# The high parts of split weights loaded by a second, rounding transfer that GpSimd issues

## The chip, the cores and the metric

The kernel runs on one core of a Trainium2 chip. A core has five engines with an instruction stream each, executed in order: TensorE (PE in the profile, its weight loads PEld), VectorE (DVE), ScalarE (ACT), GpSimd (POOL) and SyncE (SP), which in this kernel issues the transfers. Engines wait for each other on semaphores. The metric is the device time of one execution in microseconds.

## What is computed

One layer of a hybrid block over 512 latent and 256 context tokens, width 2048, in float32:

```python
h  = rms_norm(x, norm_w) * (1 + scale) + shift            # shift, scale, gate from silu(c) @ w_ada + b_ada
hc = rms_norm(ctx, norm_w) * (1 + scale_c) + shift_c      # the same from c_ctx
qkv_g, z_g, gates, q_a, k_a, v_a, z_a = split_proj(h @ w_in)      # w_in: 2048 x 6688
qkv_gc, ..., k_ac, v_ac, _            = split_proj(hc @ w_in)
# group A: 8 heads of a gated delta rule, chunks of 64, one scan forwards and one backwards,
#   first over the context, then over the latent tokens; conv of 5 taps and silu on q, k, v
o_gdn   = o_lf + flip(o_lb)
gdn_lat = rms_norm(o_gdn, gdn_norm_w) * silu(z_g)
# group B: 8 query heads, 2 key/value heads, rotary positions
attn_lat = block_attention(qa, k_all, v_all) * silu(z_a)
y = concatenate([gdn_lat, attn_lat]) @ w_out              # w_out: 2048 x 2048
out = rms_norm(x + gate * y, final_norm_w)
```

## The kernel before, in words

**Products in three passes.** The matrix products with `w_in` and `w_out` are made with operands rounded to `float32r` (F32R). To keep the accuracy, each operand is split in a high part (the value rounded to F32R) and a low part (the value less its high part), and the product is the sum of three: high x high, high x low, low x high. `hhL` and `hL` are the high and low part of `h`, `hhC` and `hC` those of `hc`, `mh` and `ml` those of the gated head outputs.

**Pieces of weights.** Weights come in pieces of 256 KB, 128 partitions x 512. A piece of `w_in` is 512 rows and 128 columns, so it is read in runs of 512 bytes; one of `w_out` is 128 rows of 512 columns, runs of 2 KB. `wpiece` allots the three tiles of a piece (`wraw`, `whi`, `wlo`, three buffers each), has SP load `wraw` (L138), and calls `split`: ACT copies `wraw` to `whi`, which rounds (L129, a CAST in the profile), and `lo_eng` subtracts (L130). `lo_eng` is VectorE (V) for 236 pieces, all but the first weights.

**Stages.** Start (to about 170 us): loading `w_ada`, the modulation, `h` and the first head's projections; its weights go through `first_weights` with GpSimd subtracting (16 pieces `wraw_w`). Scans (about 170 to 870 us): per head `gdn_scan` goes through 12 steps, and PE fills the steps' waits with the projections of the next heads, `feeding` with `proj_steps`: 24 pieces for k, 24 for q, 28 for v, 16 for the attention's keys and values (`kv`), 32 for its queries (`q0a` and so on) and 20 for gates (`z..a`). A step: `ksh` (PE, state times key), `rh` (DVE, L866), `tsh` (PE, L875), `vsh` and `vnh` (ACT, L879 and L882), `tsh` (PE, L886), `sth` (DVE, L892, the new state, which adds `sdh`, the decayed state that POOL makes, L240). Beside the scan of one head `gdn_prep` prepares the next: `cch`, `grh`, `IB`, `NTh`, `NEh` are its tiles, `cacc_k` and `cacc_q` the convolutions, `kq` and `kc` their results. Attention and gates (about 870 to 1112 us): scores, softmax and values per head, with the other 44 pieces of gate columns (`z_piece`, `fillers`, output `zl`) as PE's filler; `ptl` and `qTl` are low parts that DVE makes there. Output (about 1112 to 1302 us): four blocks of 512 columns, 16 pieces each; blocks 0 to 2 through `wpiece` (48 pieces, `wraw_wo`, output `po`), block 3 from its own tiles `rawl`, `wlh`, `wll`, loaded and split during blocks 1 and 2. `epilogue` adds each block into `yx` (`tt`, `yx`).

**What sets the order.** PE's order is that of the program, in all stages; in attention and gates DVE, ACT and POOL follow the program too. In the scans and the output a list scheduler orders the other engines from its own estimates of durations, with priorities (`first_of_all`, `soon`). A changed engine or duration of one instruction can therefore move others.

Of the kernel before, what the change touches and what calls it, by code (L numbers as in the profile page):

```python
# [9 lines left out]
F32R = mybir.dt.float32r  # L10
AF = mybir.ActivationFunctionType
ALU = mybir.AluOpType
# [56 lines left out]
def build(tc, a):  # L69
    nc = tc.nc  # L70
    V, S, G, T, SY = nc.vector, nc.scalar, nc.gpsimd, nc.tensor, nc.sync
# [4 lines left out]
    def pool(name, bufs=1, **kw):  # L76
        return es.enter_context(tc.tile_pool(name=name, bufs=bufs, **kw))
# [4 lines left out]
    wp = pool("wp", 1)  # L82
# [43 lines left out]
    def split(raw, nm, lo_eng=None):  # L126
        hi = wp.tile([128, 512], F32R, tag="whi", bufs=3, name=f"whi_{nm}")
        lo = wp.tile([128, 512], F32R, tag="wlo", bufs=3, name=f"wlo_{nm}")
        S.copy(hi, raw)  # L129
        (lo_eng or G).tensor_tensor(out=lo, in0=raw, in1=hi, op=ALU.subtract)  # L130
        return hi, lo

    def wpiece(src, nm, shape, lo_eng=None):
        raw = wp.tile([128, 512], F32, tag="wraw", bufs=3, name=f"wraw_{nm}")
        v = raw
        if shape is not None:
            v = raw.rearrange("p (a b) -> p a b", b=shape)
        SY.dma_start(v, src)  # L138
        hi, lo = split(raw, nm, lo_eng)
        if shape is not None:  # L140
            hi = hi.rearrange("p (a b) -> p a b", b=shape)
            lo = lo.rearrange("p (a b) -> p a b", b=shape)
        return hi, lo
# [10 lines left out]
    def proj_steps(col, nm, pl, pc=None):  # L154


        for kq in range(4):
            src = w_in[kq * 512:(kq + 1) * 512, col:col + 128].rearrange("(k p) c -> p k c", p=128)
            hi, lo = wpiece(src, f"{nm}_{kq}", 128, V)
            passes = [(kq * 4 + k4, n, lw, rt) for k4 in range(4)  # L160
                      for n, (lw, rt) in enumerate(hpass(kq * 4 + k4, hi[:, k4], lo[:, k4]))]

            def one(out, m, k, n, lw, rt):
                T.matmul(out, lhsT=lw, rhs=rt[m], start=k == 0 and n == 0, stop=k == KT - 1 and n == 2,  # L164
                         skip_group_check=True)

            if pc is not None and kq == 0:
                for out, m, n_ in ((pl, 0, SEQ), (pc, 1, CTX)):
                    for x in passes:
                        one(out, m, *x)  # L170
                        yield n_
                continue
            for x in passes:
                one(pl, 0, *x)
                if pc is not None:
                    one(pc, 1, *x)
                yield SEQ if pc is None else SEQ + CTX
# [196 lines left out]
    def first_weights(k):  # L374

        rows = w_in[k * 128:(k + 1) * 128]
        src = rows[:, 0:2048].rearrange("p (s c) -> p s c", s=2)[:, :, 0:256]
        hi, lo = wpiece(src, f"w0_{k}", 256)
        raw, vhi, vlo = [p0.tile([128, 128], t_, tag=i, bufs=3, name=f"{i}{k}")
                         for i, t_ in (("w0r", F32), ("w0h", F32R), ("w0l", F32R))]  # L380
        SY.dma_start(raw, rows[:, COL_V:COL_V + 128])
        S.copy(vhi, raw)
        G.tensor_tensor(out=vlo, in0=raw, in1=vhi, op=ALU.subtract)
        w0[k] = (hi[:, 0], vhi, hi[:, 1]), (lo[:, 0], vlo, lo[:, 1])
# [953 lines left out]
    def z_piece(n):  # L1338
        i, kq = zs[n // 4], n % 4
        col = (COL_ZG if i < 8 else COL_ZA - 1024) + i * 128  # L1340
        src = w_in[kq * 512:(kq + 1) * 512, col:col + 128].rearrange("(k p) c -> p k c", p=128)
        return wpiece(src, f"z{i}_{kq}", 128, V)
# [189 lines left out]
    for c in range(4):  # L1532
# [9 lines left out]
        for k in range(KT):  # L1542
            hi = op_.tile([128, 512], F32R, name=f"wlh{k}")
            lo = op_.tile([128, 512], F32R, name=f"wll{k}")
            raw = op_.tile([128, 512], F32, tag="rawl", bufs=2, name=f"rawl{k}")
# [4 lines left out]
        for t in range(4):  # L1550
# [5 lines left out]
            f = fr[:, t:t + 1]  # L1556
# [36 lines left out]
```

## Time and profile before

| | |
|---|---|
| three runs | 1307.06, 1307.14, 1307.84 us; median 1307.14 |
| the profiled execution, its span | 1304.42 us, 1302.6 us |
| TensorE clock granted | 0.993 of full speed |
| busy: PE, DVE, ACT, POOL | 1250.4, 842.5, 583.4, 141.9 us |
| traffic | 164.53 MB, mean 126 GB/s |
| the 236 pieces' raw loads, 256 KB each | landing 2.8 to 3.3 us after issue (medians by kind) |
| low parts on DVE (L130) | 0.69 us each |

The profile is one execution, in microseconds from the span's start. A row of a group names line, engine, operation, output<-inputs and shape, then how often, busy time and mean duration in ns, and after a bar the idle time of that engine just before, with what ended it. A row of a timeline has start and duration first. Tile names stand without buffer and head numbers.

### The profile page before, as it was taken

The page shows a single profiled execution, that of the slowest core. Times are in us where ns is not written, and L with a number is a line of the kernel's source. Part 1 is how long each engine was busy: PE and PEld are TensorE (multiplying, and loading weights), DVE is VectorE, ACT ScalarE, POOL GpSimd, SP SyncE. Part 2 cuts the span into 40 slices and gives each one's busy share as a digit, 9 for nine tenths or more (in the row PEclk, how much of TensorE's full clock was granted, in tenths as well). Part 3 has the DMA queues.
Part 4 walks back from the last instruction along what each step waited for, and adds up shares of the span by engine and source line. Part 5 has one row for each costly group of instructions (what it writes and reads, how often), then busy time and mean ns, then how long its engine had stood idle before and what let it go on. Part 6 is the DMA issues. An engine that isn't in the chain of part 4 may idle for free. (4 is left out here: it accounts for less than half of the span.)

```text
span 1302.6 us, 24348 instructions
## 1 busy us (share of the span) xinstructions
PE 1250.4 (96%) x9226; PEld 1018.4 (78%) x9226; DVE 842.5 (65%) x1893; ACT 583.4 (45%) x1464; POOL 141.9 (11%) x206
## 2 busy tenths in 40 slices
PE   6799999999999999999999999999999999999997
PEld 4466688888888888888888877787888888788885
DVE  5444596686867678675776646537888887555432
ACT  4222363455545454544545444535555444434211
POOL 1323100111111111111111001100000000000000
PEclk9999999999999999999999999999999999999998
DMA  9999424231332313222132443356443443475302
GB/s 354 316 326 347 133 67 107 60 67 55 74 72 62 78 47 83 67 69 57 54 83 75 106 131 110 99 164 214 149 129 114 123 140 102 161 244 190 93 33 97
DMA packets 227000, 164.53 MB, mean 126 GB/s; under 512 B 62210, under 2 KB 198491, under 8 KB 225859
## 3 DMA queue, kind: packets, MB, share of 16 engines
q1 hardware_dynamic: 226586, 162.87, 42.9%
q8 instruction: 73, 1.20, 0.4%
q14 instruction: 44, 0.36, 0.1%
q10 hardware_dynamic: 297, 0.11, 0.0%
HBM read 148.85 MB, written 14.08 MB: 125 GB/s over the span
## 5 line engine op out<-in xcount | busy, mean ns | idle before, releaser
L240 POOL TENSOR_TENSOR sdh<-sth,egl 128x256 f32<-128x256 f32 x80 | 56.9, 711 | 446.6 <-DVE sth L892 344.8
L871 ACT ACTIVATE oqh<-ksh,egsw 64x128 f32<-64x128 f32 x128 | 46.3, 362 | 92.7 <-DVE rh L866 86.4
L866 DVE SCALAR_TENSOR_TENSOR rh<-ksh,negeg,vtokh 64x128 f32<-64x128 f32 x176 | 61.2, 348 | 31.1 <-PE ksh L854 24.5
L146 PE MATMUL po<-whi_wo,mh 128*128 128x512 f32 x192 | 76.2, 397 | 0.0
L148 PE MATMUL po<-whi_wo,ml 128*128 128x512 f32 x192 | 76.1, 396 | 0.0
L147 PE MATMUL po<-wlo_wo,mh 128*128 128x512 f32 x192 | 76.1, 396 | 0.0
L1361 PE MATMUL zl<-hhL,whi_z 128*128 128x512 f32 x176 | 74.0, 421 | 0.0
L1361 PE MATMUL zl<-hhL,wlo_z 128*128 128x512 f32 x176 | 69.8, 396 | 0.0
L1361 PE MATMUL zl<-hL,whi_z 128*128 128x512 f32 x176 | 69.6, 395 | 0.0
L130 DVE TENSOR_TENSOR wlo_wo<-wraw_wo,whi_wo 128x512 fp32r<-128x512 f32 x48 | 33.0, 690 | 55.5 <-ACT whi_wo L129 55.3
L886 PE MATMUL tsh<-vsh,ktok 128*128 128x128 f32 x352 | 56.6, 283 | 6.7 <-ACT vnh L882 3.5
L886 PEld LDWEIGHTS tsh<-vsh,ktok 128*128 128x128 f32 x352 | 47.4, 190 | 16.0 <-ACT vnh L882 7.9
L129 ACT CAST whi_wo<-wraw_wo 128x512 fp32r<-128x512 f32 x48 | 29.6, 620 | 67.3 <-PE po L148 56.8
L892 DVE TENSOR_TENSOR sth<-sdh,tsh 128x256 f32<-128x256 f32 x80 | 33.6, 420 | 27.4 <-PE tsh L886 19.2
L879 ACT ACTIVATE vsh<-tsh,cch 128x128 f32<-128x128 f32 x88 | 32.2, 366 | 38.4 <-PE tsh L875 37.1
L164 PE MATMUL vl<-hhL,wlo_v 128*128 128x512 f32 x112 | 46.3, 413 | 0.0
L164 PE MATMUL vl<-hhL,whi_v 128*128 128x512 f32 x112 | 46.2, 413 | 0.0
L164 PE MATMUL vl<-hL,whi_v 128*128 128x512 f32 x112 | 45.8, 409 | 0.0
L1402 DVE SCALAR_TENSOR_TENSOR gacc<-graw,scol,gacc 128x512 f32<-128x512 f32 x60 | 44.9, 748 | 1.0
L950 ACT CAST pth<-pt 128x512 fp32r<-128x512 f32 x48 | 26.8, 585 | 40.7 <-PE pt L1289 40.7
L146 PEld LDWEIGHTS po<-whi_wo,mh 128*128 128x128 f32 x192 | 36.2, 188 | 9.5 <-ACT whi_wo L129 0.8
L148 PEld LDWEIGHTS po<-whi_wo,ml 128*128 128x128 f32 x192 | 36.2, 189 | 8.7
(540 smaller groups left out, 3890.2 us busy)
## 6 DMA issues: line engine op xcount, KB each, us to landing
wada<-in_w_ada SPq DMA_DIRECT2D x64, 512.0 KB, 8.6
graw<-in_w_ada SPq DMA_DIRECT2D x64, 256.0 KB, 3.1
wraw_wo<-in_w_out SPq DMA_DIRECT2D x48, 256.0 KB, 3.3
wraw_z<-in_w_in SPq DMA_DIRECT2D x44, 256.0 KB, 3.1
wraw_v<-in_w_in SPq DMA_DIRECT2D x28, 256.0 KB, 2.9
wraw_k<-in_w_in SPq DMA_DIRECT2D x24, 256.0 KB, 2.9
wraw_q<-in_w_in SPq DMA_DIRECT2D x24, 256.0 KB, 2.8
xs<-in_x SPq DMA_DIRECT2D x4, 1024.0 KB, 5.4
```

Source lines behind the costliest of these rows:

```text
L130: (lo_eng or G).tensor_tensor(out=lo, in0=raw, in1=hi, op=ALU.subtract)
L146: T.matmul(out, lhsT=lh, rhs=rh, start=start, stop=False, skip_group_check=True)
L147: T.matmul(out, lhsT=lh, rhs=rl, start=False, stop=False, skip_group_check=True)
L148: T.matmul(out, lhsT=ll, rhs=rh, start=False, stop=stop, skip_group_check=True)
L164: T.matmul(out, lhsT=lw, rhs=rt[m], start=k == 0 and n == 0, stop=k == KT - 1 and n == 2, skip_group_check=True)
L240: eng.tensor_tensor(out=out, in0=x, in1=y, op=ALU.mult)
L866: V.scalar_tensor_tensor(out=r[rows], in0=ks[rows, d], scalar=gsc["negeg"][rows, gcol:gcol + 1], in1=vtok[rows, p], op0=ALU.mult, op1=ALU.add)
L871: S.activation(oq[rows, v, p - 2], ks[rows, d], AF.Copy, scale=gsc["egsw"][rows, gcol:gcol + 1])
L886: T.matmul(ts[:, d], lhsT=ktok[:, p, half], rhs=vs, start=True, stop=True, skip_group_check=True)
L892: V.tensor_tensor(out=sn, in0=sd, in1=ts[:, 0:2], op=ALU.add)
L1361: T.matmul(pl, lhsT=lw, rhs=rt, start=k == 0 and m == 0, stop=k == KT - 1 and m == 2, skip_group_check=True)
L1402: V.scalar_tensor_tensor(out=acc, in0=raw, scalar=scol[:, k:k + 1], in1=acc, op0=ALU.mult, op1=ALU.add)
```

## The change

In `wpiece`, when VectorE makes the low part, the high part is no longer a copy of `wraw` by ScalarE. GpSimd issues a second transfer of the same 256 KB from the weights in DRAM into the `whi` tile, which rounds to F32R on the way. The subtraction stays on VectorE, and needs both transfers. The pieces of the first weights are as before. 236 pieces are concerned, in scans, z projections and the output's first three blocks.

```diff
     def wpiece(src, nm, shape, lo_eng=None):
         raw = wp.tile([128, 512], F32, tag="wraw", bufs=3, name=f"wraw_{nm}")
-        v = raw
+        hi = wp.tile([128, 512], F32R, tag="whi", bufs=3, name=f"whi_{nm}")
+        lo = wp.tile([128, 512], F32R, tag="wlo", bufs=3, name=f"wlo_{nm}")
+        v, u = raw, hi
         if shape is not None:
-            v = raw.rearrange("p (a b) -> p a b", b=shape)
+            v, u = [t.rearrange("p (a b) -> p a b", b=shape) for t in (raw, hi)]
         SY.dma_start(v, src)
-        hi, lo = split(raw, nm, lo_eng)
+        if lo_eng is V:
+            G.dma_start(u, src)
+        else:
+            S.copy(hi, raw)
+        (lo_eng or G).tensor_tensor(out=lo, in0=raw, in1=hi, op=ALU.subtract)
         if shape is not None:
             hi = hi.rearrange("p (a b) -> p a b", b=shape)
             lo = lo.rearrange("p (a b) -> p a b", b=shape)
```

All lines behind it move down by 6 (L886 becomes L892, L892 becomes L898). PE's order stays, but for six rows in one piece of the first output block. ACT loses 236 instructions, POOL gains as many, and the scheduler places DVE's work in the scans and the output anew.

VectorE in the scan of head 1, while head 3's q projection runs (`q3_2` and `q3_3` are its last two pieces). Before, the third piece's low part stands ahead of the convolution:

```order
L240 TENSOR_TENSOR cch2_3601<-cch2_3601,esuf_86 128x12
L130 TENSOR_TENSOR wlo_q3_2_3781<-wraw_q3_2_3778,whi_q3_2_3780 128x512
L221 SCALAR_TENSOR_TENSOR cacc_k3_3627<-craw2_1554,cvT_78,cacc_k3_3627 128x512
L221 SCALAR_TENSOR_TENSOR cacc_k3_3627<-craw2_1554,cvT_78,cacc_k3_3627 128x256
L221 SCALAR_TENSOR_TENSOR cacc_k3_3627<-craw2_1554,cvT_78,cacc_k3_3627 128x512
L892 TENSOR_TENSOR sth1_2_3687<-sdh1_2_3611,tsh1_2_3651 128x256
```

The fourth follows one step later, before `grh`:

```order
L892 TENSOR_TENSOR sth1_3_3788<-sdh1_3_3703,tsh1_3_3771 128x256
L240 TENSOR_TENSOR IB0_1638<-gqh2_3661,grh2_3500 64x4x64
L130 TENSOR_TENSOR wlo_q3_3_3813<-wraw_q3_3_3810,whi_q3_3_3812 128x512
L702 TENSOR_TENSOR grh2_3500<-grh2_3500,cch2_3601 128x768
L866 SCALAR_TENSOR_TENSOR rh1_4_3797<-ksh1_3483,negeg_85,vtokh1_2803 64x128 x2
```

Now both stand one step further down:

```order
L246 TENSOR_TENSOR IB0_1638<-gqh2_3661,grh2_3500 64x4x64 x4
L898 TENSOR_TENSOR sth1_3_3788<-sdh1_3_3703,tsh1_3_3771 128x256
L708 TENSOR_TENSOR grh2_3500<-grh2_3500,cch2_3601 128x768
L145 TENSOR_TENSOR wlo_q3_2_3780<-wraw_q3_2_3778,whi_q3_2_3779 128x512
L246 TENSOR_TENSOR grh2_3500<-gqh2_3661,grh2_3500 128x256 x2
L246 TENSOR_TENSOR grh2_3500<-gch2_3715,grh2_3500 128x128 x2
L724 STREAM_TRANSPOSE NTh2_3504<-grh2_3500 32x6x32 x3
L872 SCALAR_TENSOR_TENSOR rh1_4_3797<-ksh1_3483,negeg_85,vtokh1_2803 64x128 x2
L724 STREAM_TRANSPOSE NTh2_3504<-grh2_3500 32x6x32
L145 TENSOR_TENSOR wlo_q3_3_3812<-wraw_q3_3_3810,whi_q3_3_3811 128x512
```

`wlo_q3_2` went from ahead of `sth1_2` to behind `sth1_3`, past all of `cacc_k3`, `kq3`, `kc3`, `IB0` and the first `grh`; `wlo_q3_3` from ahead of `grh` to behind `rh1_4` and the transposes.

GpSimd at the same place, before (`vinh` and `sdh` are its only work there):

```order
L240 TENSOR_TENSOR sdh1_2_3611<-sth1_1_3573,egl_88 128x256
L671 TENSOR_TENSOR vinh2_3598<-skh2_3590,expo2_79 128x6
L240 TENSOR_TENSOR sdh1_3_3703<-sth1_2_3687,egl_88 128x256
L240 TENSOR_TENSOR sdh1_4_3800<-sth1_3_3788,egl_88 128x256
L240 TENSOR_TENSOR sdh1_5_3863<-sth1_4_3833,egl_88 128x256
```

and now:

```order
L246 TENSOR_TENSOR sdh1_2_3611<-sth1_1_3573,egl_88 128x256
L677 TENSOR_TENSOR vinh2_3598<-skh2_3590,expo2_79 128x6
L142 DMA whi_q3_2_3779<-in_w_in 128x4x128
L246 TENSOR_TENSOR sdh1_3_3703<-sth1_2_3687,egl_88 128x256
L142 DMA whi_q3_3_3811<-in_w_in 128x4x128
L142 DMA whi_v3_0_3852<-in_w_in 128x4x128
L246 TENSOR_TENSOR sdh1_4_3800<-sth1_3_3788,egl_88 128x256
L142 DMA whi_v3_1_3907<-in_w_in 128x4x128
L246 TENSOR_TENSOR sdh1_5_3863<-sth1_4_3833,egl_88 128x256
```

Each transfer waits there until PE has freed its `whi` buffer, and the `sdh` behind it waits with it.

VectorE where the output's second block begins, before:

```order
L130 TENSOR_TENSOR wlo_wo1_1_12990<-wraw_wo1_1_12987,whi_wo1_1_12989 128x512
L240 TENSOR_TENSOR tt0_0_12941<-po0_0_12572,gbc_12931 128x512
L240 TENSOR_TENSOR tt0_1_12946<-po0_1_12573,gbc_12931 128x512
L1528 TENSOR_TENSOR yx_12930<-yx_12930,tt0_0_12941 128x512
L1528 TENSOR_TENSOR yx_12930<-yx_12930,tt0_1_12946 128x512
L130 TENSOR_TENSOR wlo_wo1_2_13008<-wraw_wo1_2_13005,whi_wo1_2_13007 128x512
```

and now:

```order
L145 TENSOR_TENSOR wlo_wo1_1_12989<-wraw_wo1_1_12987,whi_wo1_1_12988 128x512
L1554 TENSOR_TENSOR wll0_13598<-rawl0_13599,wlh0_13597 128x512
L246 TENSOR_TENSOR yx_12930<-yx_12930,fwb_12932 128x512 x2
L246 TENSOR_TENSOR tt0_2_12951<-po0_2_12574,gbc_12931 128x512
L246 TENSOR_TENSOR tt0_3_12956<-po0_3_12575,gbc_12931 128x512
L1534 TENSOR_TENSOR yx_12930<-yx_12930,tt0_2_12951 128x512
L1534 TENSOR_TENSOR yx_12930<-yx_12930,tt0_3_12956 128x512
L145 TENSOR_TENSOR wlo_wo1_2_13007<-wraw_wo1_2_13005,whi_wo1_2_13006 128x512
```

`wlo_wo1_1` went behind the first two `tt` and `yx`, and `wlo_wo1_2` behind the rest of the first block's epilogue and one `wll`.

## The prediction

> **What bounds the kernel now.** I read the page first: the busy shares and the chain that ended last.
>
> ```profile
> PE 1250.4 (96%) x9226; PEld 1018.4 (78%) x9226; DVE 842.5 (65%) x1893; ACT 583.4 (45%) x1464; POOL 141.9 (11%) x206
> PE 30%; DVE 4%; issue 2%; ACT 2%; DMA 0%; SPq 0%; POOL 0%; POOLq 0%; DVEq 0%; ACTq 0%
> ```
>
> TensorE (PE) works 96% of 1302.6 us, so work taken from ScalarE (ACT), 45% busy, buys at most what PE waits for through ACT. The chain says the same: ACT 2%, DMA 0%. PE's waits, by what ended them, give that ceiling (columns: total us, times, longest).
>
> ```profile
> PE tsh L886 <- ACT vnh L882: 3.5, 6, 1.0
> PE tsh L886 <- ACT vsh L879: 3.0, 5, 0.9
> PE kvl L164 <- DVE wlo_kv L130: 2.1, 1, 2.1
> ```
>
> PE is late by ACT in the scans for 3.5 + 3.0 = 6.5 us, and by a low part once (2.1 us); no row names a `whi`. So the 236 casts cost PE almost nothing today. The groups tell what they feed (columns: busy, mean ns, idle before and its releaser).
>
> ```profile
> L129 ACT CAST whi_wo<-wraw_wo 128x512 fp32r<-128x512 f32 x48 | 29.6, 620 | 67.3 <-PE po L148 56.8 <-PE zl L1361 8.7 <-ACT tt L1529 0.9
> L130 DVE TENSOR_TENSOR wlo_wo<-wraw_wo,whi_wo 128x512 fp32r<-128x512 f32 x48 | 33.0, 690 | 55.5 <-ACT whi_wo L129 55.3
> L130 DVE TENSOR_TENSOR wlo_z<-wraw_z,whi_z 128x512 fp32r<-128x512 f32 x44 | 30.2, 688 | 13.0 <-ACT whi_z L129 13.0
> L240 POOL TENSOR_TENSOR sdh<-sth,egl 128x256 f32<-128x256 f32 x80 | 56.9, 711 | 446.6 <-DVE sth L892 344.8 <-DVE sth L890 48.2 <-DVE msh L906 23.7
> L892 DVE TENSOR_TENSOR sth<-sdh,tsh 128x256 f32<-128x256 f32 x80 | 33.6, 420 | 27.4 <-PE tsh L886 19.2 <-ACT NTq L937 2.2 <-ACT NTh L649 1.9
> L130 POOL TENSOR_TENSOR wlo_w<-wraw_w,whi_w 128x512 fp32r<-128x512 f32 x16 | 22.1, 1382 | 34.4 <-ACT whi_w L129 34.4
> ```
>
> A cast lasts 0.62 us and starts when PE frees the `whi` buffer (56.8 us of the 67.3 in the output). POOL idles before `sdh`, and `sth` waits for PE, not for `sdh`: POOL has slack.
>
> **Part 1, the casts go.** 236 x 0.62 = 146 us of ACT disappear. On PE's path lie at most the 6.5 us above, and most of those instructions stand behind copies that stay. I take -4; ends -6.5 and 0.
>
> **Part 2, the price of a high part.** It came 0.62 us after PE's release, from a raw tile already there. Now POOL issues a transfer after that release. No row shows a POOL issue; the nearest are SP's issue and transfers of equal size.
>
> ```profile
> 1149.50 0.33 SPq L138 DMA_DIRECT2D wraw_wo<-in_w_out  x1
> wraw_wo<-in_w_out SPq DMA_DIRECT2D x48, 256.0 KB, 3.3
> wraw_v<-in_w_in SPq DMA_DIRECT2D x28, 256.0 KB, 2.9
> yx<-in_x SPq DMA_DIRECT2D x16, 256.0 KB, 4.4
> wraw_w<-in_w_in SPq DMA_DIRECT2D x16, 256.0 KB, 8.3
> ```
>
> An issue takes between 0.33 us and POOL's longest instruction here, 1.38 (`wlo_w`); I take 1.0, as software work on POOL is nearer to its own instructions. Landing: at best 2.9, at worst 8.3 (a row from the start, where the DMA engines are full). I take 3.3 + (1.0 - 0.33) = 4.0 us from release. The 236 x 0.25 MB = 59 MB (MB as 2^20) more bring the share up, but from a low level:
>
> ```profile
> 170.00:870.00 700.00, 683.30 (x6176) 573.37 (x6176) 480.53 (x1219) 345.67 (x977) 92.88 (x134) 1.00 0.32 80
> 870.00:1112.00 242.00, 236.84 (x1319) 198.56 (x1318) 188.35 (x312) 116.82 (x261) 8.49 (x7) 1.00 0.46 140
> 1112.00:1246.00 134.00, 134.00 (x572) 107.10 (x571) 66.48 (x104) 50.51 (x94) 0.00 (x0) 1.00 0.51 165
> ```
>
> Columns from the third: busy us of PE, PEld, DVE, ACT, POOL, then clock, DMA share, GB/s. The output stage goes from 165 to about 165 + 48 x 0.262 MB / 134 us = 259 GB/s, a share near 0.8; the scans stay below 0.5. The issues cost POOL 148 x 1.0 us in 700 us where it works 93: hidden, but for `sdh` that queues behind a transfer waiting for its buffer, which costs some `sth` up to a us. I take +1, ends 0 and +5.
>
> [...]
>
> **Part 3, the low parts move on DVE.** This is the main term. PE's order is fixed, DVE executes in order, and in the changed order `wlo_q3_2` stands behind a whole block of convolution and `IB` work, and behind `sth1_3` and `grh`. The rows around it before:
>
> ```profile
> 330.50 0.68 DVE L130 TENSOR_TENSOR wlo_q<-wraw_q,whi_q 128x512 fp32r<-128x512 f32 x1
> ...
> 340.32 0.42 DVE L892 TENSOR_TENSOR sth<-sdh,tsh 128x256 f32<-128x256 f32 x1
> ...
> 341.23 0.75 DVE L130 TENSOR_TENSOR wlo_q<-wraw_q,whi_q 128x512 fp32r<-128x512 f32 x1
> 341.91 0.95 DVE L702 TENSOR_TENSOR grh<-grh,cch 128x768 f32<-128x768 f32 x1
> ...
> 344.81 1.57 DVE L718 STREAM_TRANSPOSE NTh<-grh 32x192 f32<-32x192 f32 x4
> 339.70 0.48 PE L164 MATMUL ql<-hhL,wlo_q 128*128 128x512 f32 x1
> 343.04 0.39 PE L164 MATMUL ql<-hhL,wlo_q 128*128 128x512 f32 x1
> ```
>
> Before, `wlo_q3_2` ran at 330.50, 9 us ahead of PE's need at 339.70. After, the work between them is the same, `grh` takes the place at 341.23 that `wlo_q3_3` leaves, and `wlo_q3_2` starts behind it at 341.23 + 0.95 = 342.2 and ends at 342.9: PE stands 3.2 us. Its high part is not what is late: its cast had ended before 330.50, so with the 4.0 us of part 2 it lands by about 335. `wlo_q3_3`, now behind the rest of `grh`, the transposes and `rh1_4`, comes after 344.81 + 1.57, less its own 0.75 that is gone from 341.23, plus 0.69 of `wlo_q3_2`, and ends 0.68 later: 347.0, with small gaps 347.3. PE needed it at 343.04: 4.3 us late in all, the 3.2 included.
>
> The head 7 order is word for word the same; head 4 is alike.
>
> ```profile
> 648.53 0.42 DVE L892 TENSOR_TENSOR sth<-sdh,tsh 128x256 f32<-128x256 f32 x1
> 651.25 0.39 PE L164 MATMUL ql<-hhL,wlo_q 128*128 128x512 f32 x1
> 413.97 0.68 DVE L130 TENSOR_TENSOR wlo_q<-wraw_q,whi_q 128x512 fp32r<-128x512 f32 x1
> 424.11 0.37 DVE L718 STREAM_TRANSPOSE NTh<-grh 32x192 f32<-32x192 f32 x1
> 421.07 0.39 PE L164 MATMUL ql<-hhL,wlo_q 128*128 128x512 f32 x1
> ```
>
> Head 7 is the same distances 308.2 us later: +4.3. In head 4, `wlo_q4_2` moves from 413.97 to behind the transposes that end at 424.48, less the 0.42 of `sth` that now follows it: it ends at about 424.7 against a need at 421.07, +3.6, of which a little may be regained: 3.4. Sum 12.0. Other pieces (kv1, q2, q5, q6) move by fewer places, each 0 to 1.5 us late: +2.5, ends 0 and +5. Bounds of part 3: 0, if PE regains each stall in later waits (it has 17 us of idle time in 700, so hardly), to 17.
>
> **Part 4, z.** There DVE works 188 of 242 us in a fixed order. A subtraction that waits for a transfer now holds the softmax work behind it (`ptl`, `qTl`), and PE waits for that. Today the casts end 13.0 us of DVE's idle time before `wlo_z`. DVE's slack of 54 us is 1.2 us a piece, and the pieces come about 5.5 us apart, so at 4.0 us only the tightest cost something: +2, ends 0 and +13 (that idle time once more, all of it passed on to PE).
>
> **Part 5, the output.** A piece takes 2.81 us (the first two rows below), and with three buffers two of them, 5.6 us, pass from a release to the next need. Landing 4.0, subtraction 0.69 and about 0.1 between them are 4.8 us: hidden, by 0.8 us, so the landing itself may grow from 4.0 to 4.8. Each us beyond that is paid once in three pieces, 48 / 3 = 16 us. Where the second block starts, DVE has other work, and the order now puts it ahead of `wlo_wo1_2`.
>
> ```profile
> 1154.41 0.69 DVE L130 TENSOR_TENSOR wlo_wo<-wraw_wo,whi_wo 128x512 fp32r<-128x512 f32 x1 [2.12 <-ACT whi_wo L129]
> 1157.22 0.69 DVE L130 TENSOR_TENSOR wlo_wo<-wraw_wo,whi_wo 128x512 fp32r<-128x512 f32 x1 [2.12 <-ACT whi_wo L129]
> 1157.83 1.28 DVE L240 TENSOR_TENSOR tt<-po,gbc 128x512 f32<-128x512 f32 x2
> 1163.59 1.28 DVE L1528 TENSOR_TENSOR yx<-yx,tt 128x512 f32<-128x512 f32 x2
> 1164.79 0.69 DVE L130 TENSOR_TENSOR wlo_wo<-wraw_wo,whi_wo 128x512 fp32r<-128x512 f32 x1
> 1164.95 0.40 PE L147 MATMUL po<-wlo_wo,mh 128*128 128x512 f32 x1
> ```
>
> It follows the `yx` that end at 1164.87 and one more subtraction, `wll` (0.69), and takes 0.69 itself: 1166.2. PE's first need of it is the row at 1164.95: +1.2; the third block, alike but with more slack, +0.8. I take +2, ends 0 and +4 while the landing holds.
>
> **Sum.** -4 + 1 + 12.0 + 2.5 + 2 + 2 = +15.5 us. The profiled execution took 1304.42 us and the median of the runs is 1307.14, 2.72 more: 1304.42 + 15.5 + 2.72 = 1322.6 us.
>
> **Rivals.** Faster: the delays of part 3 are regained because ACT's relief also lets `sth` start sooner and PE's waits for `vnh` and `vsh` go. Its place is the scans, its price the 6.5 us; it decides if `wlo_q3_2` and its like come less than 2 us late in sum. For it: DVE is only 65% busy. Against: from 334 to 341 the rows leave it no pause. Time 1307.14 - 5 = 1302. Chance 0.15.
>
> No change: the late pieces and the ACT relief cancel, 1307; chance 0.10.
>
> Much slower: transfers from POOL land in 7 us instead of 4.0 (towards the 8.3 row). Output: (7 - 4.8) x 16 = 35 us; z goes to its end, +13 instead of +2; the rest stays: 1322.6 + 35 + 11 = 1369. For it: the DMA share near 0.8 in the output, a source read in small pieces. Against: `wraw_wo` lands in 3.3 at a share of 0.51. Chance 0.13; it decides at a landing of 4.8.
>
> [...]
>
> **Chances and range.** Forecast 0.56, with its own range 1312 to 1336 (the ends of parts 3 to 5, not all at once); faster 0.15; same 0.10; much slower 0.13; held by DVE 0.06. The repeat runs spread 0.06%; about 0.2% (2.6 us) is what a measurement can tell. So faster 0.15, same 0.10, slower 0.75. To leave out 2 in 10, the range runs from 1303 to 1360.
>
> **What would show it.** In the changed trace: PE waits near 339, 421 and 648 named `ql <- DVE wlo_q`, 3 to 5 us each; no ACT CAST at `whi`; `whi` landing near 3 us from issue; the waits on `vnh` and `vsh` smaller; output still at 2.81 us a piece but for the starts of two blocks. A piece time above 2.9 us would mean the landing binds. If PE waits at none of these places, part 3 is wrong.

## The result, and the profile after

The changed kernel takes 1480.11 us (median of 4 runs, 1475.68 to 1488.21) against 1307.18: the ratio is 1.1329, 95% interval [1.1279, 1.1379]. It is slower by 173 us, outside the range of 1303 to 1360. The profiled execution has a span of 1486.4 us, 184 more than before. Its page:

```profile
PE 1309.2 (88%) x9226; PEld 1046.4 (70%) x9226; DVE 841.5 (57%) x1893; ACT 457.7 (31%) x1228; POOL 314.9 (21%) x442
PE 24%; issue 17%; DMA 14%; DVE 9%; POOL 3%; ACT 2%; SPq 1%; POOLq 0%; DVEq 0%; ACTq 0%
q0 software_dynamic: 106176, 61.88, 22.6%
```

PE does the same 9226 instructions and is busy 88% instead of 96%. On the chain that ended last, DMA went from 0% to 14%, and "issue", time in which an engine waited for nothing that the profile shows, from 2% to 17%. The new queue q0 carries the 236 transfers. Of the 184 us, 125 are idle time of PE, and in the other 59 PE is busy longer with the same instructions. PE's waits, by what ended them:

```profile
PE pt L1295 <- DVE ptl L957: 27.1, 13, 5.8
PE tsh L881 <- DVE rh L872: 25.9, 30, 2.0
PE ksh L858 <- DVE sth L898: 15.1, 16, 2.5
PE tsh L881 <- DVE UU L827: 12.3, 6, 3.7
PE ql L170 <- DVE wlo_q L145: 9.1, 4, 2.9
PE po L153 <- DVE wlo_wo L145: 7.8, 10, 2.4
PE tsh L892 <- ACT vnh L888: 2.2, 5, 0.6
PE tsh L892 <- ACT vsh L885: 1.8, 3, 0.6
```

In the kernel before, the waits for DVE's work were small:

```profile
PE tsh L875 <- DVE rh L866: 3.3, 7, 0.7
PE pt L1289 <- DVE ptl L951: 1.7, 2, 1.4
PE tsh L875 <- DVE UU L821: 1.5, 2, 0.9
```

The wait forecast at the q pieces is there (9.1 us), and the waits on `vnh` and `vsh` fell from 6.5 to 4.0 us. But most of the waiting is for DVE's ordinary work, `ptl`, `rh`, `sth` and `UU`. What held DVE stands behind the bar of its subtractions; the third row is POOL's issue:

```profile
L145 DVE TENSOR_TENSOR wlo_z<-wraw_z,whi_z 128x512 fp32r<-128x512 f32 x44 | 30.4, 691 | 93.6 <-DMA whi_z<-in_w_in 85.6 <-DMA graw<-in_w_ada 5.5 <-PE pt L1295 2.4
L145 DVE TENSOR_TENSOR wlo_wo<-wraw_wo,whi_wo 128x512 fp32r<-128x512 f32 x48 | 33.0, 689 | 74.1 <-DMA whi_wo<-in_w_out 57.3 <-DMA rawl<-in_w_out 8.4 <-PE zl L1367 4.3
L142 POOL DMA_DIRECT2D whi_z<-in_w_in x44 | 33.2, 753 | 202.8 <-PE zl L1367 129.5 <-issue 37.4 <-DVE gacc L1408 13.9
```

DVE stood 13.0 us before `wlo_z` in the kernel before, and 93.6 now, 85.6 of them for the landing of `whi_z`. Landing itself is not slow in the median (us from issue, last column):

```profile
whi_wo<-in_w_out POOLq DMA_DIRECT2D x48, 256.0 KB, 3.4
whi_z<-in_w_in POOLq DMA_DIRECT2D x44, 256.0 KB, 4.2
whi_k<-in_w_in POOLq DMA_DIRECT2D x24, 256.0 KB, 3.7
```

In order of time, one more thing shows (first POOL's queue, then DVE):

```profile
986.27 0.74 POOL L142 DMA_DIRECT2D whi_z<-in_w_in  x1 [3.92 <-issue]
990.03 0.75 POOL L142 DMA_DIRECT2D whi_z<-in_w_in  x1 [3.03 <-PE zl L1367]
998.70 0.74 POOL L142 DMA_DIRECT2D whi_z<-in_w_in  x1 [7.91 <-issue]
989.75 0.69 DVE L145 TENSOR_TENSOR wlo_z<-wraw_z,whi_z 128x512 fp32r<-128x512 f32 x1 [0.97 <-DMA whi_z<-in_w_in]
998.47 0.69 DVE L145 TENSOR_TENSOR wlo_z<-wraw_z,whi_z 128x512 fp32r<-128x512 f32 x1 [6.67 <-DMA whi_z<-in_w_in]
```

A subtraction starts at a landing (989.75, 998.47), and 0.25 us later POOL issues the next transfer, after 3 and 8 us of standing. Over all 188 pieces of `w_in` no issue began before the transfer ahead of it had landed: 59 began 0.30 to 0.31 us after that landing (e1's expectation below says 60), the others later. Of the 48 issues from `w_out`, 39 came before it. Counted from the first `kvl`, `zl` and `po` rows, the scans take 824 us instead of 718, the z stage 290 instead of 236, the output to the end 213 instead of 188.

The 59 us of longer work are for the most part PE's clock. The trace has it at full or at half speed only (1.0 and 0.5). It is at half speed in 24 stretches, each of 3.4 us or more, 122 us in all (4 stretches and 18 us in the kernel before), and PE is busy in 97 of them (10 before). In these stretches 128x512 matmuls one behind another start 0.43 us apart, outside them 0.23 (medians of 122 and 2177 in the trace of the changed kernel). By that, the 87 us more at half speed would have taken 47 at full speed: some 40 of the 59 us, an estimate. 13 of the 24 stretches come with PE's stands: there are 13 stands of more than 2.5 us between the start stage and the end, and each has a half-speed stretch that begins in it or within 1.4 us of its end. The first row is from before PE's wait for the first late q piece (348.5 to 351.2 us), the second from after it (columns as in the prediction, the clock third from last):

```profile
340.00:348.00 8.00, 8.00 (x59) 6.36 (x58) 7.56 (x17) 2.58 (x6) 2.62 (x4) 1.00 0.47 100
351.10:354.50 3.40, 3.26 (x9) 2.68 (x10) 2.25 (x8) 0.00 (x0) 0.00 (x0) 0.50 0.45 103
```

### The profile page after: what moved, and what is told of

Its sections match the earlier page's. It is cut to its first block, busy times and chain, and to the rows that moved or that the text cites. A ratio compares the mean times of both kernels' runs of the same rounds, so it can differ in the third digit from the quotient of the medians.

```text
span 1486.4 us, 24497 instructions
## 1 busy us (share of the span) xinstructions
PE 1309.2 (88%) x9226; PEld 1046.4 (70%) x9226; DVE 841.5 (57%) x1893; ACT 457.7 (31%) x1228; POOL 314.9 (21%) x442
## 3 DMA queue, kind: packets, MB, share of 16 engines
q0 software_dynamic: 106176, 61.88, 22.6%
## 4 chain that ended last, share of the span: by engine, by line
PE 24%; issue 17%; DMA 14%; DVE 9%; POOL 3%; ACT 2%; SPq 1%; POOLq 0%; DVEq 0%; ACTq 0%
DMA whi_z<-in_w_in 5%; PE zl L1367 3%; DMA whi_wo<-in_w_out 2%; PE po L153 2%; PE po L154 2%; PE po L152 2%; PE ql L170 2%; DMA rawl<-in_w_out 2%; DMA whi_k<-in_w_in 1%; PE tsh L892 1%; PE tsh L881 1%; PE kl L170 1%; POOL whi_z L142 1%; PE vl L170 1%; DVE rh L872 1%
## 5 line engine op out<-in xcount | busy, mean ns | idle before, releaser
L153 PE MATMUL po<-wlo_wo,mh 128*128 128x512 f32 x192 | 79.3, 413 | 7.9 <-DVE wlo_wo L145 7.8
L145 DVE TENSOR_TENSOR wlo_z<-wraw_z,whi_z 128x512 fp32r<-128x512 f32 x44 | 30.4, 691 | 93.6 <-DMA whi_z<-in_w_in 85.6
L1367 PE MATMUL zl<-hhL,whi_z 128*128 128x512 f32 x176 | 78.8, 448 | 0.2 <-DMA whi_z<-in_w_in 0.2
L142 POOL DMA_DIRECT2D whi_z<-in_w_in x44 | 33.2, 753 | 202.8 <-PE zl L1367 129.5
L145 DVE TENSOR_TENSOR wlo_wo<-wraw_wo,whi_wo 128x512 fp32r<-128x512 f32 x48 | 33.0, 689 | 74.1 <-DMA whi_wo<-in_w_out 57.3
L1295 PE MATMUL pt<-cmain,pr 128*128 128x128 f32 x192 | 30.8, 294 | 41.2 <-DVE ptl L957 27.1
L892 PE MATMUL tsh<-vsh,ktok 128*128 128x128 f32 x352 | 57.4, 287 | 4.1 <-ACT vnh L888 2.2
L881 PE MATMUL tsh<-rh,UU 128*128 128x128 f32 x176 | 37.8, 297 | 26.0 <-DVE rh L872 25.9
L1295 PEld LDWEIGHTS pt<-cmain,pr 128*128 128x128 f32 x192 | 23.2, 148 | 51.3 <-DVE ptl L957 32.6
L892 PEld LDWEIGHTS tsh<-vsh,ktok 128*128 128x128 f32 x352 | 48.7, 195 | 12.3 <-ACT vnh L888 6.5
L881 PEld LDWEIGHTS tsh<-rh,UU 128*128 128x128 f32 x176 | 28.5, 190 | 39.4 <-issue 15.1
L142 POOL DMA_DIRECT2D whi_wo<-in_w_out x48 | 25.5, 530 | 137.0 <-PE po L154 98.4
L153 PEld LDWEIGHTS po<-wlo_wo,mh 128*128 128x128 f32 x192 | 37.3, 194 | 21.9 <-DVE wlo_wo L145 13.5
```

The lines of the kernel that those rows point to most:

```text
L142: G.dma_start(u, src)
L153: T.matmul(out, lhsT=lh, rhs=rl, start=False, stop=False, skip_group_check=True)
L881: T.matmul(ts[:, 2], lhsT=UU[:, w], rhs=r, start=True, stop=True, skip_group_check=True)
L892: T.matmul(ts[:, d], lhsT=ktok[:, p, half], rhs=vs, start=True, stop=True, skip_group_check=True)
L1295: T.transpose(out=tp3[:, jj, qi * 128:qi * 128 + 128], in_=prs[qi][:, j * 128:j * 128 + 128], identity=ident)
L1367: T.matmul(pl, lhsT=lw, rhs=rt, start=k == 0 and m == 0, stop=k == KT - 1 and m == 2, skip_group_check=True)
```

## The experiments

Every kernel was timed against the kernel before on the same chip (medians 1305.5 to 1307.1). "Space" is the kernel's setting `dynamic_dma_scratch_size`, 1024 in the kernel before and the changed one; the expectations call it descriptor space. Where it is raised, the start stage's `hf` tile has two buffers instead of three; e10 is the control for that. In a wait list "L145" and the like shift where the edit adds lines to the kernel.

**e1, more space.** Every engine's order is that of the changed kernel.

```diff
-    nc = bacc.Bacc(..., dynamic_dma_scratch_size=1024)
+    nc = bacc.Bacc(..., dynamic_dma_scratch_size=4096)
-            hf = ... tag="hf", bufs=3
+            hf = ... tag="hf", bufs=2
```

> [...] Theory A (one at a time): in the changed kernel no transfer from w_in was issued before the one ahead of it had landed (60 of 188 started 0.30 to 0.31 us after that landing), because the space for descriptors held one such transfer; with four times the space they overlap, and of the +173 us only the late low parts and some landing remain: 1320 to 1350 us. Theory B (the transfers and their traffic are slow by themselves, and GpSimd merely follows): 1460 to 1490 us, and issues still after landings. Theory C (the order of VectorE alone costs): unchanged too, 1470 to 1490, with issues ahead of landings.

Measured 1425.58 us, ratio 1.0883 [1.083, 1.0936]. None of the three bands: 55 us come back, where theory A forecast 130 or more. POOL's issues can now overlap, and 34 of the 188 from `w_in` began ahead of the landing before them (none did with 1024):

```profile
985.00 0.74 POOL L142 DMA_DIRECT2D whi_z<-in_w_in  x1 [10.24 <-PE zl L1367]
987.80 0.74 POOL L142 DMA_DIRECT2D whi_z<-in_w_in  x1 [2.06 <-PE zl L1367]
988.17 0.69 DVE L145 TENSOR_TENSOR wlo_z<-wraw_z,whi_z 128x512 fp32r<-128x512 f32 x1 [1.50 <-DMA whi_z<-in_w_in]
```

The second is issued at 987.80, when PE frees its buffer, ahead of the first one's landing at about 988.1. So theory A holds for what made POOL stand, and is a third of the loss. By stage, the scans got 40 us back and z 23; the output, whose transfers had overlapped before, got nothing (213 and 214 us). q0's 106176 packets are 188 x 512 of 512 bytes, 48 x 128 of 2 KB and 236 x 16 of 4 bytes: each transfer has one for each run of its source and 16 more, 528 from `w_in` and 144 from `w_out`. With 1024, none of the 188 transfers of 528 packets was issued ahead of the landing before it, and 39 of the 48 of 144 packets were. How much of the space a transfer takes, no run shows; that one from `w_in` fills it at 1024 is theory A's estimate.

**e2 to e4, one stage at a time**, with the space of 1024.

```diff
-        if lo_eng is V:
+        if lo_eng is V and <the stage's names>:
             G.dma_start(u, src)
```

> The second transfer only for the 144 pieces of the scans; z projections and output have ScalarE copies as before. If the stages' losses add (scans +106 us between the first kv and the first z projection, 718 to 822): 1413 us. Theory A and B expect that alike, 1400 to 1420. Theory C, with only the low parts of the prediction's sites late: about 1322.

> The second transfer only for the 44 pieces of the z projections, where VectorE's order is unchanged. Losses that add (235 to 289 us in the stage): 1361 us, 1350 to 1370 by theories A and B. Theory C expects 1307, no change, as nothing moves there.

> The second transfer only for the 48 pieces of the output, which are 128 rows of 2 KB and were issued ahead of landings 39 times of 48. Losses that add (179 to 203 us): 1331. Theory A sees no serial issue here and puts the loss to the order and to waits behind earlier work, 1312 to 1332; theory B expects 1331; theory C about 1310.

Measured: scans 1395.53 (1.0665 [1.0634, 1.0696]), z 1353.37 (1.0347 [1.0315, 1.0379]), output 1329.15 (1.0169 [1.0145, 1.0192]). The losses of 89, 47 and 22 us sum to 158 of 173; the scans come out somewhat below their band, the other two within theirs. Theory C alone is out: z loses 47 us with VectorE's order unchanged but for one instruction.

**e5 and e6, VectorE's order and the source of the high parts crossed.** `DVE_ORDER` lists all 1893 VectorE instructions as the other kernel executes them.

```diff
+    dve = [i for i in nc.cur_bb.bb.instructions if i.engine == mybir.EngineType.DVE]
+    for x, y in zip(DVE_ORDER, DVE_ORDER[1:]):
+        tc.add_manual_dep(dve[y], dve[x].name, <no semaphore, order alone>)
```

> The kernel before, with ScalarE copies and no second transfer, but VectorE's instructions chained in exactly the changed kernel's order (PE's order stays; ScalarE's follows with a few moves). If the prediction's part 3 and the epilogue's order are right by themselves: +10 to +17 us, 1317 to 1324. If the changed order is only the scheduler's answer to later transfers and costs nothing when the high parts are early: 1305 to 1311.

> The changed kernel with descriptor space 4096 (as in e1, 1425.6 us), but VectorE's instructions chained in exactly the order of the kernel before. If VectorE standing still before a subtraction until the transfer lands is the main cost, early subtractions stand longer: 1425 to 1460. If the late low parts are the main cost, putting them back gains: 1400 or less.

e5: 1333.42, ratio 1.021 [1.0191, 1.0228]. The order alone costs 26 us with copies in place, more than forecast. Its PE waits:

```profile
PE ql L247 <- DVE wlo_q L213: 10.5, 5, 3.5
PE tsh L969 <- ACT vsh L962: 6.4, 7, 1.3
PE tsh L958 <- DVE UU L904: 5.0, 5, 2.1
PE tsh L958 <- DVE rh L949: 4.7, 13, 0.6
```

The q pieces make 10.5 of it; before, `vsh` was 3.0, `UU` 1.5, `rh` 3.3. In the profiled execution the scans are 25.5 us longer, z 1 and the output 2. ACT's order, which the scheduler makes anew, moved as well (106 of 1469 places), so a part of the 26 can be ACT's. e6: 1571.94, ratio 1.2039 [1.2008, 1.207], above both bounds given: 146 us worse than e1. Its PE waits, and one of DVE's:

```profile
PE tsh L964 <- DVE rh L955: 64.7, 35, 5.1
PE ksh L941 <- DVE sth L981: 48.0, 30, 4.5
DVE wlo_kv L228 <- DMA whi_kv<-in_w_in: 20.8, 7, 4.1
```

With the subtractions back in their early places DVE stands before them until the transfer lands, and the scan's `rh` and `sth` stand behind. So the moved order is a remedy: it costs 26 us by itself and, with three buffers, saves 146 where high parts are late. (In e6 ACT's and POOL's order moved a little too, POOL's at 23 of 442 places.)

**e7, e8: the z projections, where the program sets DVE's order.** Space 4096; e8 puts the subtraction later (the main lines of its edit):

```diff
+                if k4 == 1 and n + 1 < 4 * len(zs):
+                    lows_z.pop(0)()      # the subtraction of piece n + 1
```

> The second transfer in the z projections alone, with descriptor space 4096; control for the next kernel and for e3 (1353.4 us with 1024). In e1 the z stage took 266 us, 32 more than before: 1335 to 1342. If one transfer at a time were of no weight in this stage: 1353.

> As e7, but in the z projections the subtraction is not put into VectorE's order where the piece's loads are issued but half a piece's matmuls of TensorE later, a piece ahead of its use: the landing then passes before VectorE comes to it. If VectorE held in order by the landing is what costs: 1310 to 1322, most of e7's loss gone. If TensorE waits for the transfer itself (three buffers too few for release to landing): 1335 as e7.

e7: 1331.16, ratio 1.0197 [1.0162, 1.0232]; the space is worth 22 of z's 47 us, more than forecast. e8: 1327.33, ratio 1.0167 [1.0147, 1.0186], in neither band, almost nothing gained. Its wait is a new one (the first row is e7's, the others e8's):

```profile
PE pt L1295 <- DVE ptl L957: 14.5, 9, 4.0
PE pt L1300 <- DVE ptl L962: 1.4, 2, 1.1
PE zl L1375 <- DVE wlo_z L146: 15.4, 9, 3.1
```

`ptl` fell from 14.5 to 1.4 us, and in its place PE waits 15.4 us for low parts that now come late behind DVE's other work. So e8 could not tell its two cases apart; e15 does.

**e9 to e12, a fourth `whi` buffer.** The space is 2048 in all four.

```diff
-        hi = wp.tile([128, 512], F32R, tag="whi", bufs=3, name=f"whi_{nm}")
+        hi = wp.tile([128, 512], F32R, tag="whi", bufs=4, name=f"whi_{nm}")
```

> [...] If what remains of e1 (1425.6 us, +118) is the time from PE's release to landing, about 4 us with three buffers, most of it goes: 1320 to 1350. If it is the order of VectorE and the traffic: 1400 to 1430.

> Control: the kernel before, ScalarE copies, with four whi buffers, two hf buffers and descriptor space 2048 (unused). Copies land 0.6 us after the release, so a fourth buffer should change nothing: 1303 to 1311; more only if the scheduler's moved instructions cost by themselves.

> The second transfer in the output alone (e4, 1329.2 us, with three buffers), with four whi buffers. Its landings ran up to 6.9 us where the x, gate, final norm and last block's loads run beside them; three buffers leave 4.8, four leave 7.6. If that is the loss: 1306 to 1314. If TensorE waits for VectorE's epilogue order: 1322 to 1330.

> As e8 (z projections alone, subtraction half a piece later, 1327.3 us), with four whi buffers and descriptor space 2048. If the remaining 20 us of e8 are landings that come too late for TensorE with three buffers: 1306 to 1314. If VectorE's work itself is late: 1320 to 1328.

e9: 1329.9, ratio 1.0189 [1.0171, 1.0208]. Of 173 us 24 remain. All 236 second transfers are still made, so their traffic by itself, in this arrangement, costs 24 us at most: theory B is out too. The stand before the subtractions of z is gone though landing took nearly as long (`whi_z` 3.7 us in the median, 4.2 in the changed kernel):

```profile
L145 DVE TENSOR_TENSOR wlo_z<-wraw_z,whi_z 128x512 fp32r<-128x512 f32 x44 | 30.2, 687 | 10.6 <-issue 6.6 <-DMA whi_z<-in_w_in 2.8 <-PE zal4a L170 0.7
L145 DVE TENSOR_TENSOR wlo_wo<-wraw_wo,whi_wo 128x512 fp32r<-128x512 f32 x48 | 33.1, 690 | 56.8 <-DMA whi_wo<-in_w_out 25.6 <-DMA wraw_wo<-in_w_out 15.0 <-PE po L153 11.3
```

e10, the control: 1307.82, ratio 1.0017 [1.0008, 1.0027], no more than 0.3%. e11: 1320.1, ratio 1.0113 [1.0098, 1.0129], between its two expectations: the buffer gives back nearly 8 of the output's 22 us. PE no longer waits there for a landing (5.5 us in e4), but still for late subtractions (8.0 us), and the longest of these stands behind VectorE's other work:

```profile
PE po L153 <- DVE wlo_wo L145: 8.0, 5, 4.8
1172.19 0.69 DVE L1554 TENSOR_TENSOR wll<-rawl,wlh 128x512 fp32r<-128x512 f32 x1 [4.28 <-ACT wlh L1553]
1177.10 0.69 DVE L145 TENSOR_TENSOR wlo_wo<-wraw_wo,whi_wo 128x512 fp32r<-128x512 f32 x1
```

The high part of the subtraction at 1177.10 had landed at 1169.8; ahead of it in the order stand `wll`, which waited for ACT, and the first block's epilogue. e12: 1328.49, ratio 1.0184 [1.0162, 1.0206], as e8: its PE waits 15.5 us for `wlo_z` again.

**e13 to e15, buffer, space and order apart.** e13 is e9 with the space back at 1024, e14 is e9 with the changed kernel's VectorE order (chained as in e5), e15 is e12 with the subtraction in its old place.

> e9 (1329.9 us) with the descriptor space back at 1024, every engine's order as in e9. If the space for one transfer at a time costs whatever the buffers: 1365 to 1395 (e1 gave back 55 us). If four buffers make the serial issue harmless: 1330 to 1340.

> e9 (1329.9 us) with VectorE's instructions chained in the changed kernel's order. If the buffer did it by time alone: the order adds no more than in e5 (+26), 1330 to 1356. If e9's gain came by its order of VectorE: 1400 to 1425, as e1.

> The second transfer in the z projections alone, four whi buffers, descriptor space 2048, the subtraction where the program had it (in e12 it stood later). e9's z stage was 5 us longer than before: 1308 to 1316. If z is bound by something that four buffers don't touch: 1325 to 1331 as e7 and e12.

e13: 1364.52, ratio 1.0447 [1.0416, 1.0477], at the lower end of its first band; the space is worth 35 us with four buffers too, and again no issue from `w_in` began ahead of a landing. e14: 1350.63, ratio 1.0331 [1.0302, 1.036]: the buffer works without a change of VectorE's order, and the order adds 21 us, near e5's 26. POOL's order was not held in e14: with the fourth buffer the scheduler puts 95 of the 236 issues one to nine POOL instructions earlier, so that the gain is the buffer's together with these earlier issues. e15: 1312.53, ratio 1.0044 [1.0027, 1.006]: with four buffers the z stage loses 6 us, so 17 of e12's 23 were made by the placement of the subtraction.

The stages in the profiled executions, us from the first `kvl`, `zl` and `po` rows:

| kernel | scans | z stage | output |
|---|---|---|---|
| before | 718 | 236 | 188 |
| changed | 824 | 290 | 213 |
| e1, more space | 784 | 267 | 214 |
| e14, and a fourth buffer | 740 | 239 | 205 |
| e9, and the order that the scheduler makes for it | 726 | 241 | 203 |

In sum, from 1480 to 1306: space -55 (e1), fourth buffer at the same VectorE order -75 (e1 to e14), order -21 (e14 to e9), and 24 that remain, 15 of them in the output by its stage's time. (e14 has a space of 2048 and e1 one of 4096; no run tells these two apart.) These are steps on one path; taken in another sequence each has another size. The time that PE's half-speed clock adds is within each step and was not taken apart. No version beat the kernel before.

## Why the prediction was wrong, point by point

The step that failed is the one from "a transfer lands 4.0 us after PE's release" to "nearly nothing for PE": parts 2, 4 and 5 took 1 + 2 + 2 = 5 us for it. The landing was about as forecast. But POOL issued none of the 188 transfers from `w_in` before the one ahead of it had landed (55 us, e1), and with three buffers the landing then held DVE, which works in order, and through DVE the scans, the softmax and the output (75 us came back with a fourth buffer, e14).

- **Part 1, the casts: right.** The waits on `vnh` and `vsh` fell by 2.5 us, where -4 was taken and 0 to -6.5 allowed.
- **Part 2, the price of a high part: each term about right, what was made of them wrong.** An issue took 0.78 us of POOL in the mean from `w_in` and 0.53 from `w_out` (1.0 taken; the page calls the queue `software_dynamic`), landing 3.4 to 4.2 us in the medians of the kinds with 16 pieces or more (4.0 taken); the shortest were 2.87 us from `w_out` and 3.12 from `w_in`. What failed here is "The issues cost POOL 148 x 1.0 us in 700 us where it works 93: hidden": it took POOL to be free again after each issue. (The scans have 144 pieces, not 148.) It stood until the last transfer from `w_in` had landed; that is 55 us (e1). Nothing in the trace before showed it, since GpSimd issued no transfer there, and no rival named it. A slip that changed nothing: "the scans stay below 0.5" of the DMA share, where the prediction's own columns give 0.32 x (80 + 54) / 80 = 0.54 and the trace 0.57 (0.63 in e9).
- **Part 3, the moved low parts: right in kind, too small.** PE waited at head 3 as forecast:

```profile
351.24 0.80 PE L170 MATMUL ql<-hhL,wlo_q 128*128 128x512 f32 x1 [2.79 <-DVE wlo_q L145]
356.77 0.50 PE L170 MATMUL ql<-hhL,wlo_q 128*128 128x512 f32 x1 [0.53 <-DVE wlo_q L145]
```

  That is 3.3 us against 4.3. Heads 4 and 7 have one wait each, 2.9 and 2.8 us (3.4 and 4.3 taken), and all q waits make 9.1 us (12.0 taken). The order as a whole, by e5, costs 26 us where 14.5 and 2 for the output were taken. The output's 2 us are what e5's output stage shows; in the scans `UU`, `rh` and `vsh` came later too and were not counted.
- **Part 3's premise failed in the rest of the scans.** "Its high part is not what is late" was read at one place. DVE stood 19.6 us before `wlo_k` for landings, and 14.5 before `wlo_v`, with `rh`, `sth` and `UU` queued behind. The scans lost the most of all stages, 89 us of their own (e2).
- **Part 4, z: the step that failed most plainly.** +2 was taken, 13 the bound; alone it was 47 (e3). DVE's idle of 54 us was treated as slack for the whole stage. But the program has DVE subtract right after a piece's loads are issued, and with three buffers PE has only just freed that piece's `whi`; so a large part of the landing came back as a stand: before 30 of the 44 subtractions DVE stood for it, 2.9 us each in the mean. The bound "that idle time once more" came from a copy of 0.62 us and not from the landing that takes its place.
- **Part 5, the output: the 4.8 us were right, the landing was not constant.** In e4, the median was 3.4, but in the first two blocks landings went to 6.9 where SP's loads of x, gate, norm and last block run. Four landings of 6.3 to 6.7 us there made PE stand for 1.5 to 1.9 us each, which is what they exceed 4.8 by. In the last 11 pieces they were 2.9 to 3.6 and cost nothing. It lost 22 us, 2 taken; 8 of them go with a fourth buffer (e11), and in what remains low parts stand behind VectorE's epilogue, for up to 4.8 us where +1.2 was taken.
- **A term that is not in the sum: PE's speed.** The sum carries the matmuls' times over unchanged. In the profiled execution PE is busy 59 us longer, some 40 of them (an estimate) by the half-speed stretches, of which 13 of 24 come with its stands. If the stands bring them, which no run shows apart, a stand costs more than its own length.
- **The rivals.** "Much slower" came nearest, by the wrong mechanism: only 3 of the 236 transfers took 7 us or more to land; they were issued late, and DVE stood before them. Its 1369 was far too low. For "held by DVE" (0.06) no run speaks: 59 of POOL's stands ended 0.30 to 0.31 us after a landing, and more space took 55 us off (e1).

## What to carry to other kernels

When a copy of 0.6 us between a release and a use is replaced by a transfer of 4 us, count buffers first: with n buffers the latency must fit into the time that n - 1 pieces take, at the place in the program where the consumer stands in order, not in the mean of a stage (z alone lost 24 us with three buffers, e7, and 6 with four, e15). When transfers move to GpSimd, see whether one begins before the last has landed: here none of the 188 from `w_in` did, 59 began 0.30 to 0.31 us behind the landing, and a larger `dynamic_dma_scratch_size` took 55 us off (e1). An order that a scheduler has made can cost by itself, 26 us here; forcing the same order on the old kernel measures it apart. And when a wait of TensorE is priced, look at the clock behind it: here 87 us more of PE's work ran at half speed.

## What the hardware showed that was not expected

- GpSimd's queue stood, with everything behind it, until the last transfer from `w_in` had landed when the space was 1024 (none of 188 issued ahead of a landing, and again none in e13); with 4096, 34 of the 188 were (e1). The profile books only a part of such a stand as "issue" (37.4 us before `whi_z`): of the 59 issues right behind a landing, 23 are under "issue" and most of the others under a matmul of PE that had ended earlier.
- PE's clock went to half speed for 3.4 us or more at a time: 4 stretches before, 24 in the changed kernel, 18 in e1, 41 in e6, 7 in e5. The mean granted clock is 0.993 before, 0.973 in e1, 0.959 after, 0.945 in e6, and the same instructions keep PE busy 1250, 1289, 1309 and 1333 us. More traffic is not needed for it: e5 has no second transfer, and its runs have 0.982 to 0.987 against 0.989 to 0.992 of the kernel before beside it. Not every stand is followed by such a stretch: of the stands over 2.5 us 13 of 13 are in the changed kernel, 21 of 26 in e6; and 11 of the changed kernel's 24 stretches are at none of its 13. No run changed the stands and the clock apart from each other.
- The 62 MB more of traffic hurt SP's own loads little: in the medians the raw pieces of the output landed in 3.9 us instead of 3.3, those of z in 3.0 instead of 3.1.
